# Two transformer blocks in one launch: the opening reordered, and a fixed order by tiles where layers meet

## The chip, the cores and the metric
One core of a Trainium2 chip runs the whole program. The metric is device time in microseconds of one execution, taken as the median of three runs; a profiled execution of its own gives the trace.

## The reference
Two blocks of two layers each work on the same 256 tokens of width 1024. Each layer is a mixer and a feed-forward part, both behind a root-mean-square norm that is scaled and shifted by a modulation vector, which is computed from a condition vector by a 1024 x 6144 product:

```
mod = silu(c) @ w_ada[layer] + b_ada[layer]        # sh1, sc1, g1, sh2, sc2, g2
h = rms_norm(x, norm_mix) * (1 + sc1) + sh1
x = x + g1 * mixer(h)                              # gated delta net, then dilated attention
h = rms_norm(x, norm_ffn) * (1 + sc2) + sh2
x = x + g2 * swiglu(h, w_ffn_in, w_ffn_out)
```

The second block has a differential and grouped attention (even) and a latent attention (odd) as mixers, which also see 256 context tokens, and expert-choice experts of 16 in place of the feed-forward part. All is fp32 in and out.

## The kernel before
All activations stay on the chip. x is held as two tiles of 128 tokens by 1024. Products are made from split operands: a number is the sum of a rounded part (hi) and a rest (lo), and `mm3` (L393 to L398) adds hi·hi, hi·lo and lo·hi in one PSUM bank. Weights stream through rotating 1 MB buffers (`raw`, `load_w`, L135, issued by SyncE) and are split by `split_w`: ScalarE casts (`whi`, L387), VectorE subtracts (`wlo`, L391). With `pool_next` or `pool_share` some subtractions go to GpSimd. Three pairs of split buffers are in rotation.

The stages in order of time: opening (0 to 42 us), delta net `gdn` (to 384), feed-forward `ffn0` (to 600), dilated attention `dsw` (to 890), `ffn1` (to 1100), `even` (to 1310), its experts (to 1790), `odd` (to 1960) and its experts (to the end).

**Where two layers meet.** The last product of a layer (`dense` with `last=True`, or the second half of `ffn`) keeps back tile 1's matmuls of the last three splits until tile 0's are done. `add_out` then multiplies a bank by the gate row (L440) and adds to x (L442). `norm_T` (L335) opens the next layer tile by tile: `norm_rows` (L294) squares x on ScalarE (L299), makes the reciprocal root by `rsqrt_e` (L156 to L162: a logarithm and an exponential on ScalarE, small operations on VectorE) and scales the whole row (L302). `split_T` (L304) turns the rows by the matmul unit (L311), modulates (L326 on ScalarE or L329 on VectorE) and splits into hi (L332) and lo (L333).

**Filling.** Modulation units of later layers are generators in `self.bg`. `fill(n)` takes n steps from the first of them. A step loads 1 or 2 MB rows of `w_ada` and either multiplies them on the matmul unit (L218) or accumulates them on VectorE (L238). In `ffn0`, `fill(4)` stands before each column block but the first, and `fill(100)` at the end takes what is left.

**The opening.** Unit 0 of the first layer's modulation is computed by eight loads and eight groups of matmuls (L218). `turned_early` turns the normed x beforehand. Small vectors (gains, convolution taps) are loaded as rows by GpSimd's queue and turned by `rows_to_cols` (L178) and `runs_to_cols` (L191). `modulated` (L360) then makes hi (L371) and lo (L372, L373) of all eight column tiles, and the delta net's first products (L601 to L603) follow.

**What sets the order.** The program text gives each instruction a priority. A planner with a timing model lays the instructions into each engine's in-order queue: what its model takes as ready goes first. `keep_in_program_order(i)` pins i behind the instruction traced just before it on its engine, and `issue_after(i)` queues what a block traces on i's engine behind i. Both fix issue order only and add no wait for the end.

## Time and profile before
| | us |
|---|---|
| median of three runs (2449.21 to 2452.27) | 2452.18 |
| profiled execution | 2443.09 |
| its span, first to last instruction | 2441.3 |

The profiled execution is one run; its rows are read against its own time. Busy times are shares of a stretch, and an engine's idle time is put down to what ended it. A matmul's length has its way through the array in it, so that of several in a row the distance of the starts counts.

### The profile page before, as it was taken

The numbers are of one execution on the slowest core, as the hardware profiler recorded it, in microseconds if no ns is written. First come the engines' busy times: TensorE is split into PE (matmuls) and PEld (weight loads), VectorE is DVE, ScalarE is ACT, GpSimd is POOL, SyncE is SP. The second block draws the span as 40 slices with busy tenths as digits, with TensorE's granted clock in tenths as the row PEclk, the third lists the DMA queues.
The fourth block names the chain that finished last, engine by engine and source line by source line (L and its number), as shares of the span: only waits on it lengthen the run. The fifth ranks groups of instructions, "written<-read, shape, count | busy, mean of one in ns | idle before, by whom it ended". The sixth has DMA issues, their size and how long they took to land. (4 is left out here: it accounts for less than half of the span.)

```text
span 2441.3 us, 30277 instructions
## 1 busy us (share of the span) xinstructions
PE 2123.6 (87%) x12053; PEld 1278.1 (52%) x12053; DVE 1100.0 (45%) x2051; ACT 773.9 (32%) x1470; POOL 316.8 (13%) x334
## 2 busy tenths in 40 slices
PE   6987998998999979998988998888888987777777
PEld 3864676786677657885575222222265652222222
DVE  3777357866555575547764121212157731101111
ACT  3564344443555544435443100000047530000000
POOL 3344211112000040003411000000021010000000
PEclk8988998999999979999998999999989989989999
DMA  9657766976332356537746999999921469999998
GB/s 351 247 174 240 238 226 218 362 256 215 126 109 85 126 189 203 167 119 264 296 169 267 425 426 427 425 426 426 415 84 63 162 274 426 426 426 425 427 425 349
DMA packets 152445, 677.57 MB, mean 278 GB/s; under 512 B 15937, under 2 KB 38315, under 8 KB 113648
## 3 DMA queue, kind: packets, MB, share of 16 engines
q1 hardware_dynamic: 143072, 637.98, 67.3%
q0 software_dynamic: 6784, 36.48, 4.3%
q8 instruction: 95, 1.56, 0.3%
q10 hardware_dynamic: 2448, 1.18, 0.2%
q14 instruction: 46, 0.38, 0.0%
HBM read 667.07 MB, written 8.52 MB: 277 GB/s over the span
## 5 line engine op out<-in xcount | busy, mean ns | idle before, releaser
L391 DVE TENSOR_TENSOR wlo<-rawt,whi 128x1024 fp32r<-128x1024 f32 (+2 forms) x257 | 308.7, 1207 | 228.0 <-ACT whi L387 225.6
L387 ACT CAST whi<-rawt 128x1024 fp32r<-128x1024 f32 (+3 forms) x284 | 280.5, 995 | 313.7 <-PE mmt L398 118.9
L1872 PE MATMUL anyt<-rawb,xs 128*32 128x512 f32 x672 | 164.4, 650 | 52.0 <-DMA rawb<-in_w_exp_gate 26.7
L1858 PE MATMUL anyt<-rawb,xs 128*32 128x512 f32 x1472 | 175.2, 614 | 26.6 <-DMA rawb<-in_w_exp_up 17.3
L1832 DVE TENSOR_TENSOR y<-anyt,g 32x512 f32<-32x512 f32 (+1 forms) x120 | 66.4, 553 | 214.7 <-PE anyt L1825 206.9
L1825 PE MATMUL anyt<-rawb,hT 128*32 128x256 f32 (+1 forms) x1056 | 132.9, 491 | 21.2 <-DMA rawb<-in_w_exp_down 11.0
L398 PE MATMUL anyt<-whi,lo 128*128 128x512 f32 (+1 forms) x384 | 144.8, 379 | 1.8 <-DVE lo L333 1.8
L397 PE MATMUL anyt<-wlo,hi 128*128 128x512 f32 (+1 forms) x384 | 145.4, 380 | 1.1 <-DVE wlo L391 1.1
L1877 DVE TENSOR_TENSOR h<-anyt,h 64x512 f32<-64x512 f32 x16 | 11.1, 693 | 281.8 <-ACT h L1876 281.8
L396 PE MATMUL anyt<-whi,hi 128*128 128x512 f32 (+1 forms) x384 | 134.4, 381 | 0.4 <-ACT t L1723 0.4
L1876 ACT ACTIVATE h<-anyt 64x512 f32<-64x512 f32 x16 | 9.4, 589 | 392.4 <-PE anyt L1872 392.4
L1862 ACT ACTIVATE h<-anyt 128x512 f32<-128x512 f32 x16 | 9.6, 597 | 378.1 <-PE anyt L1858 378.1
L1872 PEld LDWEIGHTS anyt<-rawb,xs 128*32 128x32 f32 x672 | 39.3, 118 | 171.0 <-issue 100.7
L1858 PEld LDWEIGHTS anyt<-rawb,xs 128*32 128x32 f32 x1472 | 48.8, 112 | 147.1 <-issue 113.4
L1863 DVE TENSOR_TENSOR h<-anyt,h 128x512 f32<-128x512 f32 x16 | 11.1, 692 | 207.8 <-PE anyt L1858 207.8
L1825 PEld LDWEIGHTS anyt<-rawb,hT 128*32 128x32 f32 (+1 forms) x1056 | 49.5, 128 | 94.3 <-issue 65.0
L218 PE MATMUL adat<-rawt,lhs 128*32 128x512 f32 x448 | 73.6, 665 | 29.0 <-DMA rawt<-in_w_ada 24.9
L391 POOL TENSOR_TENSOR wlo<-rawt,whi 128x1024 fp32r<-128x1024 f32 (+1 forms) x27 | 67.6, 2511 | 237.7 <-ACT whi L387 196.2
L1872 PE MATMUL anyt<-rawt,xs 128*32 128x512 f32 x352 | 78.7, 596 | 10.9 <-DMA rawt<-in_w_exp_gate 7.3
L397 PEld LDWEIGHTS anyt<-wlo,hi 128*128 128x128 f32 x384 | 72.5, 189 | 20.5 <-issue 3.2
L398 PEld LDWEIGHTS anyt<-whi,lo 128*128 128x128 f32 x384 | 72.4, 188 | 16.2 <-DVE lo L333 2.2
L396 PEld LDWEIGHTS anyt<-whi,hi 128*128 128x128 f32 x384 | 71.6, 189 | 16.6 <-issue 0.8
(634 smaller groups left out, 4381.2 us busy)
## 6 DMA issues: line engine op xcount, KB each, us to landing
rawt<-in_w_ada SPq DMA_DIRECT2D x96, 1024.0 KB, 7.0
rawb<-in_w_exp_up SPq DMA_DIRECT2D x41, 2048.0 KB, 27.0
rawb<-in_w_exp_down SPq DMA_DIRECT2D x41, 2048.0 KB, 27.0
rawb<-in_w_exp_gate SPq DMA_DIRECT2D x39, 2048.0 KB, 25.6
rawt<-in_w_exp_gate SPq DMA_DIRECT2D x41, 1024.0 KB, 26.5
rawt<-in_w_ffn_in SPq DMA_DIRECT2D x40, 1024.0 KB, 7.7
rawt<-in_w_exp_up SPq DMA_DIRECT2D x38, 1024.0 KB, 27.0
rawt<-in_w_exp_down SPq DMA_DIRECT2D x31, 1024.0 KB, 27.0
```

Of the source, the lines that this page charges most:

```text
L218: nc.tensor.matmul(bank[32 * j:32 * j + 32, :], lhs[:, k, :], r[:, 0, 512 * j:512 * j + 512], start=(k == 0), stop=(k == 7))
L387: nc.scalar.copy(hi, w)
L391: e.tensor_tensor(out=lo, in0=w, in1=hi.bitcast(F32), op=OP.subtract)
L396: nc.tensor.matmul(ps, xh, wh, start=start, stop=False)
L397: nc.tensor.matmul(ps, xh, wl, start=False, stop=False)
L398: nc.tensor.matmul(ps, xl, wh, start=False, stop=stop)
L1825: nc.tensor.matmul(yb[o:o + M, c:c + n], hT[:, k, :], w[:, i * n:i * n + n], start=(k == 0), stop=(k == KT - 1), **({} if S == 2 else dict ...
L1832: nc.vector.tensor_tensor(out=ys[s][p0:p0 + CAP, 256 * q:256 * (q + n)], in0=yb[o:o + CAP, c:c + 256 * n], in1=g2[o:o + CAP, 256 * q:256 * ...
L1858: nc.tensor.matmul(b[CAP * i:CAP * i + CAP, :], lhs(k0 + j, i % 2), r[:, j, 512 * hf:512 * hf + 512], start=(k0 + j == 0), stop=(k0 + j == ...
L1863: nc.vector.tensor_tensor(out=h, in0=banks[1], in1=h, op=OP.mult)
L1872: nc.tensor.matmul(b[o:o + 32, :], lhs(k0 + j), r[:, j, 512 * hf:512 * hf + 512], start=(k0 + j == 0), stop=(k0 + j == KT - 1), tile_posit ...
L1877: nc.vector.tensor_tensor(out=h[0:64, :], in0=b[64:P, :], in1=h[64:P, :], op=OP.mult)
```

## The change
Opening: the transposes of the vectors are no longer issued where they are traced but collected in `self.turns` and pinned behind the early turn of x, and the modulation's matmuls from the second load pair on are queued behind them. The mask's load and two casts move from `gdn_consts` to behind the delta net's projections. For units of two streams (`two`) the first matmuls are pinned behind what was traced before. `pool_next` goes from 4 to 0 in `gdn` and `ffn1`, and `fill(4)` becomes `fill(6)` in `ffn0`.

Where layers meet: with `ends=True` the first tile's sums are pinned, the last tile's are deferred (`self.late`) into the following `norm_T`, which pins scale vector and first norm, then the late sums. The row is no longer scaled: a 128x128 diagonal with the reciprocal root is the moving operand of the turn. The next three weight splits, the other tile's norm, and in places the context work, the router's weights and the context keys' split are queued behind named instructions. `gate()`, which broadcasts the gate row, moves behind the projections in `even`. `ctx_norm` takes its squares and diagonals from a pool of its own, no longer from a load buffer.

```diff
+    def keep(self, ins):
+        return self.tc.keep_in_program_order(ins) if self.pin else ins
+    def after(self, *names):
+        with ExitStack() as es:
+            for n in names:
+                if n in self.behind:
+                    es.enter_context(self.tc.issue_after(self.behind[n].ins))
+            yield
...
+                    if two and k == 0:
+                        self.tc.keep_in_program_order(i)
...
+                if diag is not None:
+                    nc.tensor.matmul(tp[:, P * j:P * j + P], src[:, P * (k0 + j):P * (k0 + j) + P], diag, start=True, stop=True)
+                    continue
                 nc.tensor.transpose(tp[:, P * j:P * j + P], src[:, P * (k0 + j):P * (k0 + j) + P], self.ident)
...
+            def inv(t):
+                rs = self.inv_rms(x, t, lambda h: pool.tile([P, 512], F32, name="xsq"), rsqrt)
+                dg = pool.tile([P, P], F32, name="dg")
+                last = self.keep(nc.vector.tensor_scalar(out=dg, in0=self.ident, scalar1=rs, scalar2=None, op0=OP.mult))
+                return dg, last
+            A = self.small(KT)
+            with self.pinned() if opens else ExitStack():
+                self.keep(nc.vector.scalar_tensor_tensor(out=A, in0=sc, scalar=1.0, in1=gain, op0=OP.add, op1=OP.mult))
+                dg, last = inv(tiles[0])
+                if opens:
+                    exp = self.last_exp
+                if late:
+                    last = late()
             for t in tiles:
-                xn = pool.tile([P, D], F32, name="xn") if rows is None else rows[:, t, :]
-                self.norm_rows(x, t, xn, rsqrt)
-                self.split_T(xn, KT, t + off, hi, lo, A, sh)
+                if t != tiles[0]:
+                    with self.after("exp"):
+                        dg, _ = inv(t)
+                ends = self.split_T(x[:, t, :], KT, t + off, hi, lo, A, sh, dg)
+                if opens:
+                    if t == tiles[0]:
+                        self.behind = dict(exp=exp, add=last, hi0=ends[0], lo0=ends[1])
+                    self.behind.update(hi=ends[0], lo=ends[1])
+                    self.nbehind = 3
...
-        nc.scalar.copy(hi, w)
+        self.nbehind -= 1
+        with self.after(*("exp",) if self.nbehind == 2 else ("hi0",) if self.nbehind >= 0 else ()):
+            nc.scalar.copy(hi, w)
...
+        with self.after(*("add",) if self.nbehind == 2 else ("lo0",) if self.nbehind >= 0 else ()):
+            e.tensor_tensor(out=lo, in0=w, in1=hi.bitcast(F32), op=OP.subtract)
...
-        self.pool_share, self.pool_next = dict(ffn0=(6, 0), ffn1=(self.NEVER, 4))[key]
+        self.pool_share, self.pool_next = dict(ffn0=(6, 0), ffn1=(self.NEVER, 0))[key]
...
-                    self.fill(4)
+                    self.fill(6)
...
+                def sums(t=t):
+                    for h in range(2):
+                        last = f(h, t, banks[t][h])
+                    return last
+                if t:
+                    self.late = sums
+                else:
+                    with self.pinned():
+                        sums()
+            if key == "ffn1":
+                with self.pinned():
+                    self.late()
+                self.late = None
...
-            self.pool_next = 4
...
-                    with self.aside():
+                    with self.aside(), self.after("hi", "lo"):
                         self.ctx_attn(cp)
...
-            gate()
             hi, lo = mk_h(0)
...
             self.rate = 0
+            gate()
...
                     early = self.turned_early(x, xp)
-                    self.fill(5)
+                    for turn in self.turns:
+                        last = turn()
+                    self.fill()
+                    with self.tc.issue_after(last.ins):
+                        self.fill(4)
```

## Rows read from the trace of the kernel before
**Rows 1.** The page, busy us (share of the span) by engine.
```profile
PE 2123.6 (87%) x12053; PEld 1278.1 (52%) x12053; DVE 1100.0 (45%) x2051; ACT 773.9 (32%) x1470; POOL 316.8 (13%) x334
```
**Rows 2.** Table by stretches: busy us (instructions) PE to POOL, PEclk, DMA share, GB/s.
```profile
376.00:410.00 34.00, 26.69 (x108) 20.26 (x108) 27.60 (x43) 17.51 (x31) 4.51 (x5) 0.85 0.64 192
595.00:620.00 25.00, 17.17 (x65) 10.88 (x64) 18.68 (x48) 12.62 (x32) 6.68 (x12) 0.80 0.76 257
886.00:918.00 32.00, 23.82 (x92) 18.16 (x92) 20.77 (x35) 16.02 (x31) 13.02 (x8) 0.84 0.54 184
1095.00:1120.00 25.00, 16.23 (x76) 8.18 (x75) 18.52 (x37) 14.40 (x30) 6.10 (x3) 0.86 0.92 336
```
**Rows 3.** Timeline, opening: start, us, engine line op, [idle before <-what ended it].
```profile
25.10 1.93 PE L218 MATMUL adat<-rawt,lhs 128*32 128x512 f32 x8 [1.43 <-DMA rawt<-in_w_ada]
...
28.14 1.94 PE L218 MATMUL adat<-rawt,lhs 128*32 128x512 f32 x8
...
31.47 7.01 POOL L391 TENSOR_TENSOR wlo<-rawt,whi 128x1024 fp32r<-128x1024 f32 x3 [23.13 <-ACT whi L387]
...
33.98 1.93 ACT L371 ACTIVATE hi<-mmt,modc,smt 128x256 fp32r<-128x256 f32 x4
34.58 1.70 DVE L372 TENSOR_SCALAR t<-hi,modc 128x256 f32<-128x256 f32 x1 [0.73 <-ACT hi L371]
...
40.65 1.94 PE L218 MATMUL adat<-rawt,lhs 128*32 128x512 f32 x8 [7.66 <-DMA rawt<-in_w_ada]
...
40.97 0.34 DVE L372 TENSOR_SCALAR t<-hi,modc 128x256 f32<-128x256 f32 x1
...
41.23 0.47 DVE L373 SCALAR_TENSOR_TENSOR lo<-mmt,smt,t 128x256 fp32r<-128x256 f32 x1
...
42.51 0.58 PE L601 MATMUL mmt<-hi,whi 128*128 128x256 f32 x1
...
56.62 0.47 ACT L559 ACTIVATE cv<-mmt,cw 128x256 f32<-128x256 f32 x1 [2.66 <-PE mmt L603]
```
**Rows 4.** Timeline where the delta net meets ffn0.
```profile
382.24 1.22 DVE L391 TENSOR_TENSOR wlo<-rawt,whi 128x1024 fp32r<-128x1024 f32 x1 [1.54 <-ACT whi L387]
...
383.39 1.28 DVE L440 TENSOR_TENSOR t<-mmt,gb 128x512 f32<-128x512 f32 x2
...
384.58 3.44 DVE L442 TENSOR_TENSOR x<-x,t 128x512 f32<-128x512 f32 x2
...
390.63 1.97 PE L311 MATMUL tpt<-cst,xn 128*128 128x128 f32 x8 [4.22 <-DVE xn L302]
```
**Rows 5.** Timeline where ffn0 meets the dilated attention.
```profile
602.07 2.49 DVE L442 TENSOR_TENSOR x<-x,t 128x512 f32<-128x512 f32 x4
...
609.13 0.75 DVE L302 TENSOR_SCALAR xn<-x,smt 128x1024 f32<-128x1024 f32 x1
...
610.03 1.94 PE L311 MATMUL tpt<-cst,xn 128*128 128x128 f32 x8 [6.39 <-DVE smt L159]
```
**Rows 6.** Timeline where the dilated attention meets ffn1.
```profile
896.61 7.90 POOL L391 TENSOR_TENSOR wlo<-rawt,whi 128x1024 fp32r<-128x1024 f32 x3 [18.29 <-DVE smt L162]
896.62 2.89 DVE L302 TENSOR_SCALAR xn<-x,smt 128x1024 f32<-128x1024 f32 x1
```
**Rows 7.** Timeline where ffn1 meets even.
```profile
1103.93 3.36 PE L218 MATMUL adat<-rawt,lhs 128*32 128x512 f32 x16 [4.79 <-DMA rawt<-in_w_ada]
...
1108.59 3.67 DVE L391 TENSOR_TENSOR wlo<-rawt,whi 128x1024 fp32r<-128x1024 f32 x2 [1.97 <-ACT whi L387]
```
**Rows 8.** Table by stretches, two iterations of ffn0's first half.
```profile
436.00:460.00 24.00, 24.00 (x107) 18.52 (x107) 20.23 (x18) 10.67 (x13) 5.33 (x2) 1.00 1.03 389
460.00:485.00 25.00, 25.00 (x114) 19.38 (x113) 22.89 (x23) 10.69 (x13) 4.04 (x3) 1.00 0.94 341
```
**Rows 9.** Groups by line, VectorE's modulation steps: xcount | busy us, mean ns | idle before.
```profile
L238 DVE SCALAR_TENSOR_TENSOR adaacc<-rawt,smt,adaacc 128x1024 f32<-128x1024 f32 x42 | 57.9, 1378 | 1.3 <-DMA rawt<-in_w_ada 0.8
```
**Rows 10.** Timeline of the matmul unit: plain fp32 matmuls, and transposes at the full clock.
```profile
254.07 1.05 PE L784 MATMUL anyt<-T,BT 128*128 128x128 f32 x8
...
1117.59 1.09 PE L311 MATMUL tpt<-cst,xn 128*128 128x128 f32 x8
```

More of the change, by code (lines that the diff above doesn't have):

```diff
@@ L331, in split_T, with norm_T @@
                 m = ms[:, :n * P].rearrange("p (a b) -> p a b", a=n)
-                nc.scalar.copy(h, m)
-                nc.vector.tensor_tensor(out=l, in0=m, in1=h.bitcast(F32), op=OP.subtract)
-    def norm_T(self, x, gain, sc, sh, hi, lo, tiles, off=0, rsqrt=None, rows=None):
+                ends = nc.scalar.copy(h, m), nc.vector.tensor_tensor(out=l, in0=m, in1=h.bitcast(F32), op=OP.subtract)
+        return ends if A is not None else None
+    def norm_T(self, x, gain, sc, sh, hi, lo, tiles, off=0, rsqrt=None, opens=False):
@@ L336, in norm_T @@
         nc = self.nc
-        A = self.small(KT)
-        nc.vector.scalar_tensor_tensor(out=A, in0=sc, scalar=1.0, in1=gain, op0=OP.add, op1=OP.mult)
-        with ExitStack() as es:
-            if rows is None:
-                pool = es.enter_context(self.tc.tile_pool(reuse_waits="tile", name="xn", bufs=2, side="right"))
-            for t in tiles:
-                xn = pool.tile([P, D], F32, name="xn") if rows is None else rows[:, t, :]
-                self.norm_rows(x, t, xn, rsqrt)
-                self.split_T(xn, KT, t + off, hi, lo, A, sh)
+        late, self.late = self.late, None
@@ L398, in mm3, with dense @@
         nc.tensor.matmul(ps, xl, wh, start=False, stop=stop)
-    def dense(self, hi, lo, nk, w, cols, tiles, consumer, last=False, pairs=False, rows=None):
+    def dense(self, hi, lo, nk, w, cols, tiles, consumer, last=False, pairs=False, rows=None, ends=False):
         for ci, (n0, nn) in enumerate(cols):
@@ L429, in dense @@
                         part(i, *h)
-                if not pairs:
+                if ends and ci == len(cols) - 1:
+                    f = lambda ci=ci, t=t, b=banks[i]: consumer(ci, t, b)
+                    if i == len(tiles) - 1:
+                        self.late = f
+                    else:
+                        with self.pinned():
+                            f()
+                elif not pairs:
                     consumer(ci, t, banks[i])
```

122 lines of the change are left out of this document (72 added, 50 removed).

## The prediction
> **What bounds the kernel now.** I read the page first: the matmul unit is busy for 87% of the span [rows 1], so time is won where it stands still or runs slowly. The table by stretches tells where: over the four places where one layer hands over to the next it is busy for 26.69 of 34, 17.17 of 25, 23.82 of 32 and 16.23 of 25 us, at a granted clock of 0.80 to 0.86 [rows 2]. That is 7.3 + 7.8 + 8.2 + 8.8 = 32.1 us of standing still. The timelines of these places come next, because they show which queue held the handover up.
>
> The opening [rows 3]: the eight weight loads of the first modulation land 2.49 us apart, and the last eight matmuls of that unit end at 28.14 + 1.94 = 30.1. The modulated input is ready piece by piece from about 35, but the first matmul of the delta net starts at 42.51: ahead of it in the matmul queue stand eight matmuls of a filling unit (ada2) that wait 7.66 us for a load.
>
> The handovers [rows 4 to 7]: the queues are in order and the planner mixes next-layer work into them. At 382.24 VectorE works on a weight split of the next layer, for which it had waited 1.54 us, while a finished sum of the old layer stands behind it; two sums take 3.44 us; the turned rows begin at 390.63 after 4.22 us of idleness [rows 4]. In the next one all four sums of both tiles come before the first square, and the turn waits 6.39 us [rows 5]. In the third, three splits on GpSimd lie beside a row scaling that takes 2.89 us instead of 0.75 [rows 5, 6]. In the fourth, two splits take 3.67 us in front of the small operations of the norm, and a filling unit blocks the matmul queue for 4.79 us [rows 7].
>
> **The change, part by part.** All terms are against the profiled execution: 2443.1 us, of which the span is 2441.3. The median of the runs shown is 2452.2, so 9.1 us are added at the end.
>
> *Opening.* The vectors' transposes are pinned right behind the turned rows instead of around the last modulation matmuls; the loads for them are small, issued by 8 us. Two of them now stand before the last eight matmuls (they start at 28.14, behind an arrival due at 25.10 + 2.49 = 27.59) [rows 3]: gain 0.5. Two casts and one load of a mask move behind the delta net's projections, where nothing waits for them for over 100 us: nothing, or 0.5 off VectorE's path. The ada2 unit's first matmuls are pinned behind everything traced before them, here the first two column blocks of the delta net. What is late next is the modulated input. Its first hi piece came at 33.98; 0.5 earlier, and about 1 more because the turns and casts between are gone, is 32.4, and the first lo piece takes one subtraction and one multiply-subtract after it, 0.34 + 0.47 [rows 3]. The first matmul can then start at 34 to 35 rather than 42.51. But VectorE must do eight such pairs, 6.5 us, and now also the first four weight splits (pool_next is gone), 4 x 1.22 = 4.9 us [rows 4]: together 11.4, done at about 44, and the last quarter of the block's 96 matmuls follows, about 3 us. So VectorE paces the first block, and its end, which is where ScalarE takes the first column at 56.62 [rows 3], comes at about 47, 9 to 10 us earlier. In exchange GpSimd no longer splits beside VectorE, where the same subtraction took 1.70 us [rows 3]. The eight ada2 matmuls come back in a busy stretch (1.94 at the low clock, about 1 at the high). I take -8; ends -3 (half of the 7.66 comes back as a wait for weights) and -10. Behind the pinned matmuls on their queue stands only the third column block; two of the five load buffers stay held longer, and SP's later weight loads queue behind them: that is what the -3 allows for.
>
> *Handovers.* The sums of the first tile, the scale vector and the norm's small operations are pinned in that order on VectorE; the last tile's sums come behind the first tile's diagonal; three splits queue behind the exponential, the last sum and the first tile's hi and lo. The row scaling, 0.75, becomes a 128x128 diagonal (about 0.2 by its quarter of the columns and the fixed part), and the turn becomes a matmul with it. Worked out for the first place: the last 18 matmuls are held for tile 1; at 0.22 each (107 in 24 us, [rows 8]) tile 0 is whole about 4 us before the end at 384.3. From the first sum's end to the turn it took 384.58 to 390.63, 6.05 us; without the second sum and the slowing (3.44 - 0.62, [rows 4, 5]) and with the diagonal that is 2.7, plus one product of 0.64 (1.28 for two). So tile 0 can be turned as soon as the held matmuls end, 6 us earlier. What is late next is VectorE: tile 1's sum 1.3, three splits 3.7, small operations 1.0, modulation 2.7, lo parts 2.6: 11.3 us against 36 matmuls and 16 turns of about 10 us. VectorE waits in that order for ScalarE's square, logarithm and exponential with all splits behind it. So 2 to 3 us of idleness stay at each place. -32.1 + 4 x 2.5 = -22. In the third place the matmul unit also waits on a gather of the context stream, which nothing reorders; in the fourth the pinned ada2 matmuls (3.36) and the row gain's broadcast, moved behind the projections, stay work to be done: neither was idle time, so neither is counted. The moved broadcast carries two GpSimd products, four matmuls and two copies past the projections into the attention, where ScalarE is not the bound; 0, at most +2. Ends of this part: -11 if VectorE's order gives back half, -32 if nothing stays, and -7 more if the matmuls of these places run at full clock (eight turns take 1.94 against 1.09, twice at each place [rows 5, 10]).
>
> *Turning by a matmul.* Eight plain fp32 matmuls of 128x128 take 1.05 us and eight transposes 1.09 [rows 10]: 0. Here a rule speaks against the change: the Trainium skill, "TensorE: Matmul & The Clock Gate", Terms, says that the transpose mode is four times faster for FP32. By it 80 blocks would each cost three more times 0.136, some 33 us, and the sum would end at +9. The rows do not show that.
>
> *Fill of six instead of four in ffn0.* 25 steps of modulation and tables are taken in four iterations of six and a rest instead of five of four with five left for the end. An iteration takes 24 to 25 us, with transfers at 1.03 and 0.94 of the queue's share and VectorE at 20.23 and 22.89 [rows 8]. Two more steps are 2.1 MB and four VectorE operations of 1.38 [rows 9], 5.5 us. Then 10.49 MB per iteration at the best rate shown, 389 GB/s, are 27.0 us, and VectorE needs 26 to 28: +1.5 us for each of four iterations, +6. Below: 0, if the slack of the load buffers carries it. Above: at the 341 GB/s of the other row, 30.8 us each against 25.5, +21. What stood at the end (accumulations, matmul, broadcast) leaves the second handover; its matmul time is moved, not saved. The Trainium skill's "DMA: Bandwidth & Descriptors", Where 436 GB/s comes from, gives 435 for the fabric and about 358 for the HBM side, which would bind; by the former this term is 0, by the latter +15 and the sum -15. The 389 of rows 8 is above the latter, so the measurement decides.
>
> *Splits in ffn1.* Four go from GpSimd to VectorE, +4.9 there, with the contention gone (2.89 against 0.75): in the handover's term.
>
> Sum: -8 - 22 + 6 = -24, 2419 for the profiled execution, 2428 for the median. All later stages (experts, odd layer) depend on the layers before and load their rings from there, so the shift passes to the end.
>
> **The rivals.**
> 1. *VectorE takes the place of the waits.* For it: 11.3 us against 10 in each handover, no slack. Against: it had idle time there. Handovers -11, opening -5, fill +6: -10, 2442.
> 2. *Everything goes, and the clock with it.* For it: the half clock of rows 2. Handovers -32 and about half of the clock's 7, opening -10, fill +6 or less: -40, 2412.
> 3. *The fill starves ffn0* (the slower side). Price 4 x (10.49 MB / rate - 25.5 us). It outweighs the 30 us of gains from a rate below about 318 GB/s; at 300 it is +38 and the sum +8, 2460. For it: the stretch runs at a full share already. Against: 389 was reached there.
> 4. *Turns at four times the price*, +9, 2461: rows 10 speak against it.
> 5. *The planner issues in the same order anyway*, 2452: the pins leave it no choice on VectorE, so hardly.
>
> **How the numbers follow.** Forecast 0.55 (2419 to 2438), rival 1 0.20, rival 2 0.11, rival 3 0.08, rival 4 0.02, rival 5 0.04. Likeliest time 2428. Range 2412 to 2450: it takes in rivals 1 and 2 and leaves out most of 3 and 4. A difference of 0.2%, 4.9 us, is about what a measurement of this kernel can tell from none. Faster: the forecast, rival 2 and most of rival 1, 0.84; within 0.2%: rival 5 and the rest, 0.07; slower: 0.09.
>
> **What would show it.** First delta net matmul before 36 us, no ada2 matmul ahead of it; the first block's end paced by VectorE. At each handover the first turn within 2 us of the last held matmul, the busy time in the four stretches up by 4 to 6 us each. In ffn0 iterations of 26 to 28 us and matmuls waiting for loads of w_ffn_in. I am wrong if iterations stay at 25 (then rival 2's side), if they reach 30 (rival 3), or if the handovers' idleness reappears before the second split.

## The result and the profile after

The changed kernel takes 2512.9 us (median; 2507.0 to 2517.4) where before takes 2451.8: a ratio of 1.0257, interval 1.0236 to 1.0278. It is 2.6% slower, on the other side of the forecast and outside its range. The profiled execution spans 2511.0 us against 2441.3, 69.7 more. That is more than the 61 between the medians, because the profiled execution of before ran 9 us below its median.

Where they went shows in the table by stretches, cut at the first product of each layer (columns as in [rows 2]). Before: delta net, first and second half of ffn0, dilated attention (dsw), second half of ffn1, even layer:

```profile
42.50:395.00 352.50, 308.08 (x1949) 243.04 (x1946) 215.76 (x386) 171.59 (x324) 114.30 (x99) 0.92 0.66 223
395.00:535.30 140.30, 139.19 (x651) 107.87 (x650) 110.39 (x114) 62.72 (x79) 22.21 (x15) 0.99 0.87 309
535.30:614.70 79.40, 71.57 (x305) 54.80 (x303) 50.56 (x66) 33.18 (x48) 17.98 (x16) 0.94 0.63 218
614.70:906.30 291.60, 270.20 (x1286) 201.12 (x1284) 173.21 (x416) 150.83 (x357) 33.11 (x36) 0.93 0.36 118
...
1037.00:1118.40 81.40, 72.63 (x320) 53.73 (x320) 43.56 (x58) 35.74 (x49) 7.96 (x7) 0.96 0.49 173
1118.40:1327.00 208.60, 189.73 (x1060) 138.24 (x1058) 137.83 (x248) 87.56 (x178) 56.63 (x55) 0.95 0.64 243
```

The same six stretches of the changed kernel:

```profile
42.40:404.00 361.60, 314.06 (x1968) 246.22 (x1968) 204.48 (x384) 169.47 (x321) 112.12 (x97) 0.91 0.64 214
404.00:584.10 180.10, 159.91 (x680) 117.55 (x681) 129.43 (x130) 64.08 (x83) 24.40 (x17) 0.90 0.80 277
584.10:657.10 73.00, 68.38 (x291) 53.90 (x290) 31.52 (x44) 30.87 (x44) 16.27 (x16) 0.96 0.41 147
657.10:970.30 313.20, 282.43 (x1305) 208.44 (x1304) 173.95 (x427) 150.39 (x355) 27.39 (x34) 0.91 0.37 120
...
1102.70:1178.00 75.30, 67.66 (x294) 54.95 (x293) 37.90 (x51) 29.20 (x41) 4.22 (x5) 0.94 0.37 130
1178.00:1393.40 215.40, 191.33 (x1104) 139.85 (x1103) 139.97 (x255) 93.45 (x186) 60.78 (x57) 0.96 0.67 256
```

Read the lengths: +9.1, **+39.8**, -6.4, **+21.6**, -6.1, +6.8, and 5 in what is not shown. The first half of ffn0 does 4% more matmuls and takes 28% longer: the matmul unit stands for 20.2 us where it stood for 1.1, and its granted clock falls from 0.99 to 0.90, between the two levels of 1.2 and 2.4 GHz. The dilated attention is edited only by a queueing and in the handover at its end, and still grows by 21.6.

The four handovers, in windows of the lengths of [rows 2]:

```profile
385.00:419.00 34.00, 27.92 (x124) 21.14 (x123) 23.84 (x42) 17.24 (x33) 4.39 (x5) 0.95 0.36 114
637.00:662.00 25.00, 20.38 (x74) 14.91 (x73) 14.69 (x31) 11.14 (x24) 8.18 (x13) 0.80 0.60 189
950.00:982.00 32.00, 26.37 (x118) 21.48 (x117) 18.92 (x39) 15.66 (x32) 0.00 (x0) 0.93 0.46 144
1155.00:1180.00 25.00, 17.36 (x72) 14.51 (x71) 13.51 (x28) 9.02 (x24) 2.46 (x2) 0.80 0.52 188
```

6.1 + 4.6 + 5.6 + 7.6 = 24.0 us of standing still against 32.1: the fixed order does what it says, by 8 us and not by 22.

The opening, VectorE and the matmul unit (timeline, against [rows 3]; L431 and L432 are the two steps of a piece of lo, the lines between are left out):

```profile
30.74 1.22 DVE L453 TENSOR_TENSOR wlo<-rawt,whi 128x1024 fp32r<-128x1024 f32 x1 [12.54 <-ACT whi L448]
...
31.96 1.22 DVE L453 TENSOR_TENSOR wlo<-rawt,whi 128x1024 fp32r<-128x1024 f32 x1
34.14 1.23 DVE L453 TENSOR_TENSOR wlo<-rawt,whi 128x1024 fp32r<-128x1024 f32 x1 [0.96 <-ACT whi L448]
...
35.45 0.68 DVE L274 TENSOR_TENSOR brow<-adat,brow 128x512 f32<-128x512 f32 x1
...
38.87 0.48 DVE L432 SCALAR_TENSOR_TENSOR lo<-mmt,smt,t 128x256 fp32r<-128x256 f32 x1
...
41.76 0.48 DVE L432 SCALAR_TENSOR_TENSOR lo<-mmt,smt,t 128x256 fp32r<-128x256 f32 x1
...
42.38 0.55 PE L679 MATMUL mmt<-hi,whi 128*128 128x256 f32 x1 [5.08 <-DVE lo L432]
...
85.89 1.50 PE L246 MATMUL adat<-rawt,lhs 128*32 128x512 f32 x12
```

No filling matmul stands ahead of the delta net any more, but its first product comes at 42.38, as before (42.51). Three weight splits stand on VectorE in front of the sum of the modulation (L274), whose matmuls ended at 28.9. The first piece of lo is done at 39.35, the fifth at 42.24, and the product follows the fifth. And the pinned filling matmuls run at 85.89.

### The profile page after: what moved, and what is told of

The parts are those of the page before. It is cut to its first block, busy times and chain, and to the rows that moved or that the text cites. A ratio compares the mean times of both kernels' runs of the same rounds, so it can differ in the third digit from the quotient of the medians.

```text
span 2511.0 us, 30407 instructions
## 1 busy us (share of the span) xinstructions
PE 2161.2 (86%) x12133; PEld 1303.6 (52%) x12133; DVE 1087.8 (43%) x2059; ACT 772.6 (31%) x1470; POOL 298.7 (12%) x326
## 5 line engine op out<-in xcount | busy, mean ns | idle before, releaser
L453 DVE TENSOR_TENSOR wlo<-rawt,whi 128x1024 fp32r<-128x1024 f32 (+2 forms) x265 | 316.4, 1203 | 271.1 <-ACT whi L448 255.4
L460 PE MATMUL anyt<-whi,lo 128*128 128x512 f32 (+1 forms) x384 | 148.7, 388 | 0.0
L1956 PE MATMUL anyt<-rawt,xs 128*32 128x512 f32 x352 | 80.4, 596 | 11.5 <-DMA rawt<-in_w_exp_gate 7.8
L459 PE MATMUL mmt<-wlo,hi 128*128 128x512 f32 (+1 forms) x192 | 77.6, 405 | 2.0 <-DVE wlo L453 2.0
L246 PE MATMUL adat<-rawt,lhs 128*32 128x512 f32 x448 | 65.2, 642 | 15.7 <-DMA rawt<-in_w_ada 11.9
```

What stands on the lines that cost most here:

```text
L246: i = nc.tensor.matmul(bank[32 * j:32 * j + 32, :], lhs[:, k, :], r[:, 0, 512 * j:512 * j + 512], start=(k == 0), stop=(k == 7))
L453: e.tensor_tensor(out=lo, in0=w, in1=hi.bitcast(F32), op=OP.subtract)
L459: nc.tensor.matmul(ps, xh, wl, start=False, stop=False)
L460: nc.tensor.matmul(ps, xl, wh, start=False, stop=stop)
L1956: nc.tensor.matmul(b[o:o + 32, :], lhs(k0 + j), r[:, j, 512 * hf:512 * hf + 512], start=(k0 + j == 0), stop=(k0 + j == KT - 1), tile_posit ...
```

## The experiments

All ratios are to the kernel before on the same chip; 0.1% is 2.45 us. The lengths of the stretches come from one trace each: e15_last_rows has, by the programs, exactly the matmul order of before up to ffn1, and its lengths still differ by up to 2.2 us, so that less than this is not read. "Same order" is the share of the dsw layer's matmuls that stand, by the two programs, in the order of before, counted by matching the longest equal runs first. A and B are the two theories that each expectation names.

| kernel | ratio (95%) | delta net | ffn0, 1st half | dsw | same order in dsw |
|---|---|---|---|---|---|
| before | 1 | 352.5 | 140.3 | 291.6 | 1 |
| changed | 1.0257 (1.0236-1.0278) | 361.6 | 180.2 | 313.2 | 0.47 |
| e1_fill4 | 1.0174 (1.0145-1.0204) | 359.0 | 151.7 | 310.4 | 0.47 |
| e2_noopens | 1.0198 (1.0169-1.0226) | 363.7 | 172.1 | 302.1 | 0.62 |
| e3_opening | 1.0190 (1.0162-1.0218) | 346.3 | 174.1 | 317.4 | 0.48 |
| e4_rowscale | 1.0276 (1.0245-1.0306) | 369.2 | 178.9 | 311.1 | 0.48 |
| e5_order_off | 1.0085 (1.0061-1.0109) | 346.6 | 148.7 | 301.8 | 0.63 |
| e6_handovers | 1.0076 (1.0059-1.0092) | 345.7 | 151.4 | 309.9 | 0.47 |
| e7_pool4 | 1.0247 (1.0227-1.0266) | 365.5 | 174.8 | 314.7 | 0.47 |
| e8_free | 1.0060 (1.0039-1.0081) | 342.9 | 151.7 | 304.3 | 0.65 |
| e9_rows_off | 1.0049 (1.0032-1.0066) | 354.2 | 142.5 | 288.5 | 0.99 |
| e10_rows_tables | 1.0018 (1.0007-1.0030) | 353.1 | 141.0 | 290.9 | 0.99 |
| e11_tables | 1.0033 (1.0017-1.0048) | 345.3 | 142.2 | 295.7 | 0.60 |
| e12_rows_pins | 1.0058 (1.0037-1.0080) | 350.5 | 152.8 | 296.6 | 0.97 |
| e13_nopin_fill | 1.0231 (1.0204-1.0258) | 350.0 | 176.9 | 311.8 | 0.47 |
| e14_loads | 1.0127 (1.0100-1.0153) | 347.7 | 146.2 | 309.4 | 0.47 |
| e15_last_rows | 1.0012 (0.9995-1.0028) | 354.7 | 140.7 | 289.5 | 1.00 |
| e16_last_diag | 1.0030 (1.0012-1.0049) | 345.2 | 144.6 | 298.1 | 0.60 |
| e17_fill6_only | 1.0161 (1.0138-1.0184) | 351.8 | 169.8 | 305.9 | 0.65 |
| e18_raw6 | 1.0137 (1.0121-1.0154) | 356.5 | 158.4 | 299.0 | 0.65 |

**Undone one at a time: e1_fill4, e2_noopens, e3_opening, e4_rowscale.**

```
 e1_fill4
-                    self.fill(6)
+                    self.fill(4)
```


> The changed kernel (2512.9 us) with four filling steps instead of six in each ffn0 iteration; all else of the change stays. Theory A (the fill starves ffn0): ffn0, from the first turned block of its norm to that of the next layer, goes from 250.5 us (399.56 to 650.05) back to about 225, the waits for the whi casts at 452 and 480 (4.25 and 5.89 us) go, the granted clock between 450 and 550 rises from 0.83 to 0.88 to above 0.95, and the time falls by 20 to 30 us, to 2483 to 2493. Theory B (the six steps only move work that has to be done anyway, and the loss is in the order at the handovers): what ffn0 gains comes back in the next layer, where the remaining steps then stand, and the time stays within 6 us of 2512.9.

0.83% of the 2.57 come back; ffn0's first half loses 28.5 of its 40 us. Not all: 11 remain, with a wait of 4.20 us at 451.9 for a cast (see e9 to e11). A.

```
 e2_noopens (three calls)
-    self.norm_T(x, ..., hi, lo, (0, 1), opens=True)
+    self.norm_T(x, ..., hi, lo, (0, 1))
```


> The changed kernel without the fixed order on VectorE at the handovers: the norm's operations are not pinned and nothing is queued behind the exponential, hi and lo; the diagonal, the late sums, the opening and six filling steps stay. Theory A (the fixed order works, 21 us of waits over the four handovers where there were 32): these waits come back and the time rises by 5 to 15 us, to 2518 to 2528. Theory B (the fixed order is what costs, since it holds other work behind it): the time falls by over 10 us, below 2503.

B: 0.6% faster without the fixed order. Its waits come back in part (ffn1's second half 80.5 instead of 75.3), and more is won behind them: dsw 302.1 instead of 313.2.

```
 e3_opening
-                    for turn in self.turns:
-                        last = turn()
-                    self.fill()
-                    with self.tc.issue_after(last.ins):
-                        self.fill(4)
+                    self.fill(5)
 ...
-                    if two and k == 0:
-                        self.tc.keep_in_program_order(i)
 ...
+            self.pool_next = 4
```


> The changed kernel with the opening of the kernel before: vectors turned where they are loaded, filling modulation not queued behind, its first matmuls not pinned, the first four weight splits on GpSimd, the mask loaded early; handovers and six filling steps as changed. Theory A (VectorE now makes three weight splits ahead of the modulation vector, 35.45 instead of 30.97 us, so the new opening gives back what it gains, and the eight modulation matmuls taken out of the wait at 30 to 40 us cost time in the delta net): the first turned block of ffn0 comes 6 to 10 us earlier than at 399.56 and the time falls to 2503 to 2508. Theory B (the opening is a gain that the later parts hide): the time rises by 3 to 8 us, to 2516 to 2521.

A, and more: the first product of ffn0 comes 15.7 us earlier (388.2), 0.67% in time. With the old opening the delta net is 6 us shorter than before; the new one gives away 15.

```
 e4_rowscale
-                last = self.keep(nc.vector.tensor_scalar(out=dg, in0=self.ident, ...))
+                last = self.keep(nc.vector.tensor_scalar(out=dg, in0=x[:, t, :], ...))
 ...
-                    nc.tensor.matmul(tp[...], src[...], diag, start=True, stop=True)
+                nc.tensor.transpose(tp[...], src[...], self.ident)
```


> The changed kernel with rows scaled by VectorE and turned by transposes, as before, in the new fixed order; the diagonal and its matmuls go. Theory A (a turn by an fp32 matmul takes two matrix passes of 0.11 us where the transpose takes one of 0.14, and 80 of them took 26.8 us of the matmul unit's time): 80 x (0.22 - 0.14) = 6 us less matmul time, against 0.75 - 0.2 = 0.55 us more on VectorE at each of 10 scalings, mostly beside other work: the time falls by 2 to 7 us, to 2506 to 2511. Theory B (the turns are hidden behind VectorE's modulation, which needs longer): within 2 us of 2512.9, or up to 5 slower for the scaling.

The matmul time falls as A has it, and by more; the total is as B: 1.0276 is not apart from 1.0257. In the changed kernel 64 turns by diagonal, in e4_rowscale 64 transposes (groups by line, xcount | busy us, mean ns | idle before):

```profile
L348 PE MATMUL tpt<-dg,x 128*128 128x128 f32 x128 | 21.5, 331 | 19.5 <-DVE dg L384 16.9 <-DVE t L368 2.6
```

```profile
L350 PE MATMUL tpt<-cst,xn 128*128 128x128 f32 x64 | 12.0, 341 | 23.8 <-DVE xn L383 10.1 <-DVE smt L330 6.4 <-ACT h2i L371 3.7
```

64 turns are 128 records: an fp32 matmul is two. 9.5 us more for the unit, but with the rows scaled it waits 23.8 us ahead of them instead of 19.5.

**What is left when several parts go: e5_order_off, e6_handovers, e7_pool4, e8_free.**

```
 e5_order_off: the edits of e1_fill4, e2_noopens and e3_opening
```


> Three parts of the change undone at once: four filling steps in ffn0, the opening of before, no fixed order at the handovers. What stays: turns by a matmul with a diagonal, the late sums, the gate of the even layer behind its projections, no splits on GpSimd in ffn1. Theory A (the three parts cost by themselves, one beside the other): undone one at a time they gave ratios to before of 1.0174, 1.0198 and 1.0190 where the whole change has 1.0257, so together 0.0083 + 0.0059 + 0.0067 = 0.021 and a ratio of 1.005 is left, 2464 us on the scale where before has 2451.8. Theory B (the loss sits in what stays, the diagonal and the moved gate, and the parts only shift it): the ratio stays above 1.013, over 2483 us.

A within the error of the three differences that it adds (1.005 expected, 1.0085 measured): the parts add up roughly, 1.7% together where they gave 2.1% one at a time, and 0.85% sits in what stays.

```
 e6_handovers: the edits of e1_fill4 and e3_opening
```


> The fixed order at the handovers, with what stands around it, but with four filling steps and the opening of before: the handover part of the change alone. Theory A (the fixed order costs in the layers behind each handover more than the 17 us that it gains at the four places, because context attention, tables and routing are queued behind hi and lo): 1.0257 - 0.0083 - 0.0067 = 1.011, 2478 us on the scale of 2451.8, with the dsw layer at 310 us or more against 291.6 and the handovers (ffn0 out, ffn1 out) at 75 against 79.4 and 81.5. Theory B (the fixed order gains when the loads of ffn0 are no longer late): a ratio of 0.99 to 1.0, 2427 to 2452.

Neither: 1.0076, the same as e5_order_off without the order. The order gains some 5 us at two of its places (ffn0's second half 74.4 against 79.3, ffn1's 76.9 against 81.6) and dsw takes 309.9 instead of 301.8.

```
 e7_pool4
             self.accv = dp
+            self.pool_next = 4
```


> The changed kernel with the first four weight splits of the delta net back on GpSimd, nothing else. Theory A (three splits of 1.22 us on VectorE stand ahead of the sum of the first modulation, which therefore comes at 35.45 instead of 30.97 us): the sum comes at 31 to 32, the first delta net matmul at 36 to 38 instead of 42.38, and the time falls by 4 to 6 us, 2507 to 2509. Theory B (the splits compete for VectorE's access, the subtraction then takes 1.7 to 2.3 us instead of 0.35 as before, and the modulation is late again): the first matmul stays within 2 us of 42.4 and the time within 3 us of 2512.9; then the 16 us that the old opening is worth lie elsewhere in the delta net, in the pinned filling matmuls.

B. The modulation's sum comes at 28.56, earlier than before, yet the delta net begins at 41.55:

```profile
28.56 0.69 DVE L274 TENSOR_TENSOR brow<-adat,brow 128x512 f32<-128x512 f32 x1 [9.73 <-PE adat L246]
...
32.07 1.28 ACT L727 ACT_TABLE_LOAD   x1
...
34.41 1.92 ACT L430 ACTIVATE hi<-mmt,modc,smt 128x256 fp32r<-128x256 f32 x4
...
36.42 2.63 DVE L431 TENSOR_SCALAR t<-hi,modc 128x256 f32<-128x256 f32 x2
```

Now ScalarE is late (casts and a table load ahead of the hi pieces), and beside GpSimd's splits two subtractions take 2.63 us, as before, where one took 1.70 [rows 3].

```
 e8_free: as e6_handovers, and
-                    with self.aside(), self.after("hi", "lo"):
+                    with self.aside():
 ...
-                with self.after("hi", "lo"):          # keys of the even layer
-        with self.after("lo"):                        # routing
 ...
+            gate()                                    # ahead of the projections again
```


> The handover part alone, as in e6_handovers, with three of its queueings taken out: context attention, the split of the even layer's keys and the routing are no longer queued behind hi and lo, and the gate of the even layer stands ahead of its projections again. Pinned norms, late sums, queued weight splits and diagonals stay. Theory A (these queueings are what costs behind the handovers): dsw falls from 310 to about 295 us, the even layer from 217 to about 209, and the time is 20 to 25 us below that of e6_handovers, at a ratio of 0.993 to 1.003. Theory B (they do not matter; the pinned order itself or the lower clock behind it costs): within 6 us of e6_handovers.

Between the two: 5.6 us less in dsw and 0.16% in time, where the interval overlaps with that of e6_handovers. The queueings are a part at most.

**The square of diagonal and table pin: e9_rows_off, e10_rows_tables, e11_tables** (the fourth corner is e5_order_off), **and e12_rows_pins.** The change also pins the matmuls of dsw's bias tables, a part of the filling work, behind what is traced before them. Neither the section on the change nor the forecast's sum has this pin.

```
 e9_rows_off: the edits of e5_order_off and e4_rowscale
```


> As e5_order_off (four steps, the opening of before, no fixed order at the handovers; ratio 1.0085), and in addition rows scaled by VectorE and turned by transposes in place of the diagonal matmuls. In this program the planner puts the matmuls of the delta net and of the dsw layer in the order of before again (with the diagonal they are mixed otherwise). Theory A (the diagonal costs little by itself, but it makes the planner mix the layers otherwise, and in dsw that mix is worse): dsw goes from 301.8 to 292 to 294 us, the ratio to 1.003 to 1.005. Theory B (the mix does not matter, only the turns' own time of some 6 us over the kernel does): dsw stays above 298 us and the ratio above 1.0055.

A: dsw 288.5, ratio 1.0049, with an interval that just touches that of e5_order_off.

```
 e10_rows_tables: as e9_rows_off, and
-            self.tc.keep_in_program_order(nc.tensor.matmul(ps[0:H, 0:384], ...))
+            nc.tensor.matmul(ps[0:H, 0:384], ...)
```


> As e9_rows_off, and the bias tables' matmuls no longer pinned, so that the planner takes them at the end of the delta net again, and the matmuls of ffn0 stand in the order of before. Theory A (the pin moves the tables from the end of the delta net into ffn0's iterations, where a load buffer is held for them and VectorE and the queue of filling work are late: the 4.2 and 1.9 us of waits there): the first part of ffn0 goes from 148.6 to 140 to 142 us, 6 to 8 us below e9_rows_off, a ratio of 1.000 to 1.002. Theory B (the loss in ffn0 comes from the diagonal or from the drop of the clock, not from the tables): within 2 us of e9_rows_off in ffn0.

B for ffn0, which shortens by 1.5 us only. The ratio falls to 1.0018 all the same, though the two profiled spans are alike (2452.7 and 2453.0): the profiled run of e9_rows_off was the fastest of its five, 7 us below their median, so this 0.3% has no place in the traces.

```
 e11_tables: as e5_order_off, and the edit of e10_rows_tables
```


> As e5_order_off with the diagonal kept, and only the bias tables' matmuls no longer pinned: the fourth corner of the square of diagonal and pin. Theory A (two separate causes): ffn0's first part as short as in e10_rows_tables, 140 to 143 us, dsw as long as in e5_order_off, 300 to 303, ratio 1.005 to 1.007. Theory B (the diagonal is behind both): ffn0's first part stays at 147 us or more.

A for ffn0: with the diagonal the pin costs 6.5 us there (148.7 to 142.2), with the rows 1.5; dsw (295.7) and the ratio come out below what A expected. In the changed kernel the tables' matmuls run at 433.95, inside ffn0's iterations; before, the first two of the six ran at 385.6, at the end of the delta net. With the diagonal the delta net is shorter by 8 us (345 against 353) and dsw longer by 5 to 13.

```
 e12_rows_pins: the edits of e8_free and e4_rowscale
```


> The handover part with rows scaled and transposed: fixed order, late sums and queued splits stay, four steps, the opening of before, gate in its old place, context attention, keys and routing not queued behind hi and lo. The planner's order in dsw is nearly that of before. Theory A (the fixed order is worth the 10 to 17 us that it won at the four places, once the mix behind them is left as it was): dsw 292 to 296 us, ratio 0.994 to 0.999, the first version faster than before. Theory B (what is won at the places is lost behind them in any case): ratio 1.002 or more.

B: 1.0058. With dsw in almost the order of before (296.6) the fixed order still does not pay; ffn0's first half takes 152.8. The table pin is still in this kernel. The fixed order at all handovers with scaled rows and without that pin was not run.

**What was still open: e13_nopin_fill, e14_loads, e15_last_rows, e16_last_diag.**

```
 e13_nopin_fill
-                    if two and k == 0:
-                        self.tc.keep_in_program_order(i)
```


> The changed kernel, with only the pin taken from the first matmuls of each filling unit of the second modulation. Theory A (the pin holds these matmuls until 85.89 us, their two loads occupy two of the delta net's load buffers until then, and its own weights come late: a transfer rate of 106 GB/s between 60 and 80 us against 253 before, waits of 1.83 and 1.70 us, and a burst of filling work at 361 GB/s afterwards): the rate there is over 230 GB/s again, the delta net takes 346 to 352 us instead of 361.6 and the time falls by 8 to 15 us, to 2498 to 2505. Theory B (the pinned transposes and the splits on VectorE are the cost, as a first modulation vector at 35.45 shows): the delta net stays above 357 us and the time within 5 us of 2512.9.

A for the stretches. The filling matmuls now run when their loads arrive, at 39.95 and 42.50 instead of 85.89, and the delta net takes 350.0 instead of 361.6. The stretch from 60 to 80 us, in the order before, changed, e13_nopin_fill:

```profile
60.00:80.00 20.00, 20.00 (x172) 18.43 (x172) 15.16 (x27) 11.04 (x21) 6.21 (x8) 1.00 0.70 253
```

```profile
60.00:80.00 20.00, 16.57 (x138) 15.99 (x137) 12.34 (x21) 8.33 (x16) 3.71 (x5) 1.00 0.35 106
```

```profile
60.00:80.00 20.00, 19.53 (x166) 17.77 (x166) 17.85 (x42) 12.17 (x21) 5.87 (x7) 1.00 0.65 226
```

With the buffers occupied, 106 GB/s instead of 253, and the matmul unit waits 3.4 of 20 us for casts and splits of weights. In time, less than A has it: 0.26% by the ratios, whose intervals overlap.

```
 e14_loads: the edits of e1_fill4, e13_nopin_fill and e10_rows_tables
```


> The changed kernel without the pin of the filling matmuls, with four filling steps, and without the pin of the bias tables: the three parts that are suspected of keeping load buffers occupied; the fixed order, the diagonal, the turned vectors, the moved gate and the queueings behind hi and lo stay. Theory A (most of the loss is late loads): 2512.9 - 20 (fill) - 12 (pin) - 8 (tables) = 2473, a ratio of 1.006 to 1.011, and in ffn0's first part 141 to 145 us. Theory B (the three share one cause and overlap): a ratio above 1.014.

1.0127, between the two ranges: half of the loss goes with the three parts that keep load buffers occupied. Delta net (347.7) and ffn0 (146.2) are nearly at or below before, dsw is at 309.4.

```
 e15_last_rows: the edits of e8_free, e4_rowscale and e10_rows_tables;
                opens=True and late sums only from ffn1 to the even layer
```


> The kernel before with the fixed order at the last handover alone, from ffn1 to the even layer: sums and norm pinned, three splits queued, no splits on GpSimd in ffn1, rows scaled and transposed; up to there the planner's order is that of before. Theory A (the fixed order is worth its 4 to 6 us per place where what follows isn't mixed anew): ffn1's second part 75 to 77 us instead of 81.5, the even layer 208 to 211, ratio 0.997 to 0.999. Theory B (the even layer is mixed otherwise and gives it back): even layer 212 to 216 us, ratio 0.9995 to 1.002.

B: 1.0012, interval 0.9995 to 1.0028, no difference. ffn1's second half takes 82.6 us, no less than before: there the sums of both tiles are pinned ahead of the norm, which may be why.

```
 e16_last_diag: as e15_last_rows without the edit of e4_rowscale;
                late sums at every handover
```


> As e15_last_rows with turns by the diagonal and the late sums at every handover (the delta net then takes 345 us instead of 352.5, the dsw layer some 4 to 10 us more). Theory A (the diagonal is a gain of 7 us in the delta net that dsw gives back in part): ratio 0.996 to 1.000. Theory B (dsw gives back all and more): ratio 1.001 to 1.004.

B: 1.0030. The 7 us that the delta net gains go in dsw (298.1) and ffn0 (144.6).

**The price of the fill by itself: e17_fill6_only, e18_raw6.**

```
 e17_fill6_only, in the kernel before
-                    self.fill(4)
+                    self.fill(6)
```


> The kernel before with six filling steps in each ffn0 iteration instead of four, nothing else. Theory A (the price is the starved iterations themselves, with or without the rest of the change): iterations of 31 to 36 us instead of 24 to 27, ffn0's first part 165 to 175 us instead of 140, 3 to 7 us of it given back in its second part, time up by 20 to 30 us, ratio 1.008 to 1.012. Theory B (the price comes from the fixed order and the pinned tables beside the steps): iterations of 26 to 28 us and a ratio of 1.002 to 1.004, as the sum had it.

A, and beyond: **this one line costs 1.61%, some 39 us.** Iterations of 29.9, 36.0, 31.3 and 34.9 us; ffn0's first half +29.6, dsw +14.3. First half of ffn0 and dsw:

```profile
394.20:564.10 169.90, 154.59 (x665) 114.15 (x664) 124.50 (x127) 61.84 (x79) 22.60 (x15) 0.92 0.83 286
...
641.90:947.90 306.00, 273.78 (x1282) 203.60 (x1280) 171.58 (x414) 148.85 (x351) 33.01 (x37) 0.91 0.37 122
```

```
 e18_raw6: as e17_fill6_only, and
-        ..., self.more_raw(5, key=key):
+        ..., self.more_raw(6, key=key):
```


> As e17_fill6_only, with six instead of five more load buffers in the two ffn layers. Theory A (loads wait for buffers that VectorE gives back late; the rate of the transfers is a result, not the cause): ffn0's first part 4 us or more shorter than in e17_fill6_only. Theory B (the transfers are the bound at 300 to 350 GB/s, or VectorE's own work per iteration is): within 3 us of e17_fill6_only.

```profile
398.80:557.20 158.40, 147.92 (x664) 110.29 (x663) 126.10 (x127) 61.40 (x79) 22.30 (x15) 0.97 0.88 313
```

A: with one buffer more ffn0's first half is 11.5 us shorter, the rate rises from 286 to 313 GB/s and the clock from 0.92 to 0.97. 18 us over before remain there. The planner also lays this half out anew for the buffer (0.82 of its matmuls stand in the order of e17_fill6_only), so the 11.5 are not the buffer's alone for certain. In time the gain is 0.24%, inside the intervals.

## Why the prediction was wrong

**The fill (+6 forecast, some +39 measured).** The step that failed is the rate: 10.49 MB "at the best rate shown, 389 GB/s". The first wide Silu of an iteration marks its length (timeline of ScalarE). Before, the first and the fifth:

```profile
407.73 0.60 ACT L477 ACTIVATE t<-anyt 128x512 f32<-128x512 f32 x1 [0.77 <-PE anyt L398]
...
509.17 0.60 ACT L477 ACTIVATE t<-anyt 128x512 f32<-128x512 f32 x1 [0.58 <-PE anyt L398]
```

After:

```profile
420.47 0.60 ACT L546 ACTIVATE t<-anyt 128x512 f32<-128x512 f32 x1
...
559.31 0.60 ACT L546 ACTIVATE t<-anyt 128x512 f32<-128x512 f32 x1 [0.58 <-PE anyt L460]
```

101.4 / 4 = 25.4 us against 138.8 / 4 = 34.7, where I had 27.0 and at the most 30.8. 10.49 MB in 34.7 us are 302 GB/s. Rival 3 had this mechanism, and its formula gives 4 x (34.7 - 25.5) = 37: the likeliest case was the wrong one, and its chance of 0.08 came from the 389. The four iterations in the table by stretches (before, changed, e17_fill6_only, e18_raw6):

```profile
407.70:509.20 101.50, 101.19 (x441) 75.87 (x441) 84.34 (x81) 42.87 (x50) 15.75 (x9) 1.00 0.96 347
```

```profile
420.50:559.30 138.80, 119.53 (x458) 83.84 (x457) 104.53 (x98) 42.26 (x50) 17.41 (x12) 0.88 0.87 307
```

```profile
406.90:539.00 132.10, 117.62 (x457) 82.22 (x456) 100.50 (x95) 42.50 (x51) 18.00 (x11) 0.91 0.88 310
```

```profile
411.50:532.30 120.80, 111.19 (x457) 78.51 (x457) 102.32 (x95) 42.10 (x50) 17.70 (x11) 0.97 0.94 339
```

The first failure is the choice of 389, the best of single stretches. Over the iterations of before the mean was 347, with the transfers at 0.96 of their share. At 347, 10.49 MB are 30.2 us, an estimate from these rows: about half of the 9.3 us that an iteration grew by. With one buffer more an iteration takes just that (120.8 / 4 = 30.2). The second failure is that the rate does not hold. With six steps it falls to 307, while the transfers' share is 0.87 and VectorE is busy for 104.5 of 138.8 us, so that neither is full. The waits of the load queue (engine, line, waited for: us in total, times, longest) show what is short, before and after:

```profile
SPq L135 <- DVE wlo L391: 67.9, 24, 5.4
SPq L135 <- DVE adaacc L238: 56.0, 18, 17.2
```

```profile
SPq L136 <- DVE wlo L453: 84.1, 24, 15.5
SPq L136 <- DVE adaacc L268: 73.5, 23, 9.8
```

In both the queue stands for 0.88 of the half until VectorE gives a buffer back (123.9 of 140.3 us, 157.6 of 180.1): buffers pace the loads, and weights of ffn0 and rows of the filling share them in one order. With six steps a wait for a split's buffer grows to 15.5 us where 5.4 was the longest. ScalarE's casts wait longer for weights of ffn0 (before, then after), and the matmul unit, which had no such wait before, waits for these casts:

```profile
ACT whi L387 <- DMA rawt<-in_w_ffn_in: 9.3, 3, 6.2
```

```profile
ACT whi L448 <- DMA rawt<-in_w_ffn_in: 20.4, 3, 14.6
...
PE anyt L458 <- ACT whi L448: 10.1, 2, 5.9
```

e18_raw6 speaks for the buffers in 11.5 of 29.6 us. That the other 18 are the bytes at the old mean rate is an estimate; no run separates them from VectorE's order and the clock. The HBM limit of about 358 GB/s (the Trainium skill, "DMA: Bandwidth & Descriptors", Where 436 GB/s comes from) would have given +15 by my sum, nearer than +6. The traces do not show it as the limit: the kernel before moves 425 GB/s from 1440 to 1540 us, and e18_raw6 moved the rate of the half from 286 to 313 GB/s, below that limit.

**The opening (-8 forecast, 0 at the first matmul and some +9 to +15 behind it).** Three steps failed. "The first matmul can then start at 34 to 35" let it follow the first piece of lo. By the program its wait is for the count that VectorE reaches with the fifth, and it starts 0.15 us behind that piece: 42.38 after 42.24 in the changed kernel, 41.55 after 41.40 in e7_pool4. Before, the fifth was done at 41.23 + 0.47 = 41.70 [rows 3], so the filling matmuls held the start (42.51) back by under 1 us, not by the wait of 7.66 that the forecast wanted to win. The forecast also put the first four weight splits beside the eight pairs; three stand ahead of the modulation's sum, which came at 35.45 instead of 30.97. Returned to GpSimd (e7_pool4) they uncover ScalarE's table load and the slowed subtractions, so that what is late next holds the start at 42 in either case. And "two of the five load buffers stay held longer" was the right place with a wrong size. The range left 5 us for it (-3 instead of -8); the buffers were held for 45 us, and without the pin the delta net is 11.6 us shorter (e13_nopin_fill).

**The handovers (-22 forecast, -8 at the places, nothing in time).** The first turn came 2.8, 4.0, 1.8 and 6.0 us after the last matmul, three of them near the 2.5 that I left. But the sum left one wait at each place, and there is a second behind the first turn (first place, the matmul unit):

```profile
399.56 2.05 PE L348 MATMUL tpt<-dg,x 128*128 128x128 f32 x16 [2.83 <-DVE dg L384]
...
403.95 0.50 PE L458 MATMUL anyt<-whi,hi 128*128 128x512 f32 x1 [2.34 <-ACT hi L371]
```

So 6.1, 4.6, 5.6 and 7.6 us stand where 2.5 each were left. The last place failed by a line that I had not followed: in ffn1 the sums of both tiles are pinned at once and stand ahead of the norm, timeline of VectorE:

```profile
1163.57 0.69 DVE L509 TENSOR_TENSOR t<-mmt,gb 128x512 f32<-128x512 f32 x1 [4.69 <-PE mmt L460]
...
1168.28 0.69 DVE L511 TENSOR_TENSOR x<-x,t 128x512 f32<-128x512 f32 x1
...
1170.47 0.29 DVE L384 TENSOR_SCALAR dg<-cst,smt 128x128 f32<-128x128 f32 x1
```

The shorter second halves (-6.4, -6.1) are also in part moved work, not waits: 10 accumulations went into ffn0's first half, and the 32 matmul records of the filling unit (3.36 us for 16 of them in [rows 7]) into the even layer, which grew by 6.8. In time the fixed order is worth 0.0009 of the ratio without the other parts (e5_order_off and e6_handovers, intervals overlapping), costs 0.6% with them (e2_noopens), and makes no difference where it stands alone, at the last handover (e15_last_rows). The gains at the places are shown; that the layers behind give them back is seen in the lengths, not proven step by step.

**The turns (0 forecast).** Rows 10 were misread: the eight records of L784 in 1.05 us are four matmuls, since a plain fp32 matmul shows as two records and a transpose as one. The price is 0.26 us a turn at the full clock (16 records in 2.05 us, at 399.56) against 0.136, about twice; 80 turns cost some 10 us more of the unit. The diagonal, an eighth of a row's columns and not a quarter, took 0.29 us where the forecast had 0.2. The four times of the Trainium skill's "TensorE: Matmul & The Clock Gate", Terms, were nearer to the truth than my row in that a matmul costs more, but twice too high. In time the price was hidden (e4_rowscale): with scaled rows the unit stood 4.3 us longer ahead of the turns. That this is the whole reason was not shown.

**What the sum had no term for: the dilated attention (+21.6).** That "the shift passes to the end" took the layers behind an edit as fixed. The planner lays them out anew for every edit. In the kernels with 0.97 to 1.00 of dsw's matmuls in the old order it takes 288.5 to 296.6 us; at 0.60 to 0.65, 295.7 to 305.9; at 0.47 to 0.48, 309.4 to 317.4. In e17_fill6_only no line of dsw is changed, and it is 14.3 us longer. In the changed kernel the unit's clock there is 0.91 instead of 0.93 and it stands for 30.8 instead of 21.4 us, 11.6 of them where the routing's short operations are left with few matmuls beside them. The routing's stretch before, with 7.8 us, and after:

```profile
850.00:870.00 20.00, 12.20 (x66) 9.27 (x66) 17.76 (x51) 11.79 (x26) 8.82 (x9) 0.69 0.31 106
```

```profile
920.00:945.00 25.00, 13.37 (x48) 10.50 (x48) 14.60 (x28) 5.50 (x11) 16.67 (x17) 0.58 0.60 201
```

The step from 0.63 to 0.47 is the queueing behind hi and lo (e2_noopens, e8_free), that from 1 to 0.6 the diagonal (e5_order_off against e9_rows_off) or the fill (e17_fill6_only). Order and length go together over the twenty kernels, with a small overlap (296.6 us at 0.97, 295.7 at 0.60). The middle step hangs on the way of counting: by the longest common subsequence both lower groups stand at 0.78 to 0.80, and only the step from 0.97 or more to the rest remains. That the order alone makes the length was not tried, nor which of the shifted instructions matter, so the cause of these 21.6 us stays open.

**What of the 2.57% is accounted for.** Taken out one at a time, fill, opening and fixed order give 0.83 + 0.67 + 0.59 = 2.1%; taken out together 1.72 (e5_order_off). Of the 0.85 that stay, diagonal and table pin are 0.67 (e10_rows_tables); 0.18 is left for the moved gate, the late sums and the splits of ffn1, which were not separated. Of the 1.72, the 0.6 of the fixed order shows only beside the other parts. The forecast's -30 us of gains were 8 us of waits at four places, none of them in the time. No version ran faster than the kernel before.

## What to carry to other kernels

Before filling more work into a stretch, ask which buffers it borrows and who gives them back: a load queue in order with shared buffers turns a small delay of the freeing engine into a late weight, and the best rate of a single stretch, 389 GB/s, says little about it where the mean of the same iterations was 347. A pin on one queue also holds what that instruction has already taken, here two load buffers for 45 us. Where a planner lays out the program, every local edit is also an edit of all later layers: look at their order in the new program first, and give that a range of its own. Before a start is forecast, look up in the program which piece the first product waits for: here it was the fifth, not the first.

## What was not expected of the hardware

A plain fp32 matmul of 128x128 shows as two records, a transpose as one. At the full clock eight matmuls take 2.05 us and eight transposes 1.09. In ffn0's first half, where the matmul unit had waits of 2 to 6 us, its granted clock fell from 0.99 to 0.90, and waits of 20.2 us went with 20.7 us more of busy time, for some 4% more matmuls.
